# First loads of a convolution/FFN layer on eight cores: a plain first weight tile, 256-token x pieces in turn with weights, and dummy matmuls between

## The chip, the cores and the metric

The kernel runs on all eight cores of one Trainium2 chip. Each core does one layer for one prompt sequence of 2048 tokens and for 16 decode tokens; the cores exchange nothing. The time of a run is that of its slowest core. It is given in microseconds (us). Most executions agree within 0.3%. Some fall into a slow state, in which one die (cores 0 to 3 or 4 to 7) has a lower granted clock. "Granted clock" is the share of TensorE's full clock that the profile shows; "half clock" below is a record of 0.5. Slow runs are left out of every comparison below: medians, ratios and intervals use fast runs alone. PE is TensorE's matmul side in the profile.

## The reference, cut to what matters

The weights are the same for all cores, x is not. The part that matters here is the first feed-forward block, above all its first two products.

```python
D_MODEL, SEQ, D_FF = 1024, 2048, 2816

def swiglu(x, w_gate, w_up, w_down):
    return (jax.nn.silu(x @ w_gate) * (x @ w_up)) @ w_down

def trunk_layer(x, ctx_a, ctx_b, ...):
    x = layer_norm(ALPHA * x + 0.5 * swiglu(x, f1_wg, f1_wu, f1_wd), ...)
    m, new_a, new_b = token_mixers(x, ctx_a, ctx_b, ...)   # needs the carried conv state
    x = layer_norm(ALPHA * x + m, ...)
    x = layer_norm(ALPHA * x + 0.5 * swiglu(x, f2_wg, f2_wu, f2_wd), ...)
    return x, new_a, new_b
```

## The kernel before

All data lie in HBM as f32; matmuls read bf16. In this kernel the loads of x and of the weights that GpSimd issues cast on their way ("casting queue" below). The loads that SyncE issues ("plain queue") land as f32; where bf16 is needed, they land in a stage (a part of the tile `sb_hT` that is not yet in use), and VectorE (DVE) and ScalarE (ACT) cast from there.

The feed-forward block works by weight tile `f` of 128 hidden columns. One tile is 1 MB at the source: 8 KB per partition, the gate half first, then the up half. A tile meets 1024 tokens in two groups of 512; each group is 8 matmuls for the gate and 8 for the up product.

```python
def u_group(idx, b, f, g):                 # [cut to its operations]
    P.op("pe", lambda e: mm(e, 0, bg), reads=[("ring", s, 0)] + xtoks(tok0, n), writes=pst(bg))
    P.op("pe", lambda e: mm(e, 1, bu), reads=[("ring", s, 1)] + xtoks(tok0, n), writes=pst(bu))
    P.op("act", ... Silu ..., writes=[("sg", q)])
    P.op("dve", ... multiply ..., writes=[("hT", f, gi)])
```

Side work (later loads, constants) is woven between the groups by `merge`. It runs a side entry first and then pops as many groups as the gap to the next entry allows:

```python
def merge(items, side):
    credit = 0.0
    for th, gap in side:
        th()
        credit += gap
        while credit >= 1.0 - 1e-9 and items:
            items.pop(0)()
            credit -= 1.0
```

The start of the kernel before, and the load of the carried convolution state (960 KB, plain queue), which waits for a token of tile 1:

```python
first_x(0)              # plain queue: tokens 0..255, 1 MB, cast by DVE and ACT
first_x(1)              # plain queue: tokens 256..511
fetch_wgu(0, 2)         # casting queue: weight tile 0 in two halves
fetch_wgu(1, 2)
fetch_wgu(2)
fetch_xt(0)             # casting queue: tokens 512..1023, 2 MB at the source
fetch_wgu(3)
# [cut] 10 dummy matmuls on zeros, then
u_group(0, 0, 0, (0, 256, 0))
u_group(0, 0, 0, (256, 256, 0))
u_group(1, 0, 1, (0, 512, 0))
u_group(2, 0, 2, (0, 512, 0))
for f in range(3):
    u_group(f, 0, f, (512, 512, 1))
    fetch_wgu(f + NSLOT)
u_group(3, 0, 3, (0, 512, 0))
u_group(3, 0, 3, (512, 512, 1))
# [cut] sample_state(), its first entry:
P.op("sp", lambda e: e.dma_start(out=CA, in_=scat...), reads=[("hT", 1, 1)], writes=["CA"] + ...)
ev = [(0, ss[0]), (1, consts), (18, ss[1]), (22, consts2)] + [(0.5 + 3.0 * i, ... load_wd(0, i)) ...]
merge(up_items(0, 0)[8:], side)
```

## Time and profile before

The first three runs took 1218.16 to 1219.61 us, median 1219.1 us.

| what | value | from |
|---|---|---|
| span of the cores | 1214.0 to 1218.2 us | list of cores |
| PE busy on the slowest core | 98% | page, part 1 |
| start of uninterrupted matmuls, core 1 | 30.2 us | chain of waits |
| real matmul work done by then | 10.4 us | 64 matmuls; 216 ns per 512 columns, 109 per 256 |

The next lines are the chain that ended last on core 1, the slowest, within the first 120 us (start, duration, what). It is read from top to bottom in time.

```profile
4.38 25.60 DMA sb_xT<-xtb
29.98 0.25 issue
30.23 89.87 PE ps L522 x402
```

The 512-token x load, issued at 4.38 us, lands at 29.98 us. From then on PE does not stop. The waits of PE on the same core over the whole run (total us, times, longest) show what else stands in its way; L522 is the matmul of `u_group`, L1115 the dummies, L890 a transpose in the mixer.

```profile
PE ps L522 <- DMA sb_ring<-wgu: 7.5, 2, 7.1
PE ps L522 <- DMA sb_xT<-xtb: 3.2, 1, 3.2
PE ps L1115 <- DVE sb_dgb L1079: 2.4, 1, 2.4
PE ps L890 <- ACT sb_wring L880: 1.1, 1, 1.1
PE ps L522 <- DVE sb_hT L529: 0.5, 1, 0.5
```

All but the last two lie in the first 30 us.

### The profile page before, as it was taken

The page shows a single profiled execution, that of the slowest core. Times are in us where ns is not written, and L with a number is a line of the kernel's source. Part 1 is how long each engine was busy: PE and PEld are TensorE (multiplying, and loading weights), DVE is VectorE, ACT ScalarE, POOL GpSimd, SP SyncE. Part 2 cuts the span into 40 slices and gives each one's busy share as a digit, 9 for nine tenths or more (in the row PEclk, how much of TensorE's full clock was granted, in tenths as well). Part 3 has the DMA queues.
Part 4 walks back from the last instruction along what each step waited for, and adds up shares of the span by engine and source line. Part 5 has one row for each costly group of instructions (what it writes and reads, how often), then busy time and mean ns, then how long its engine had stood idle before and what let it go on. Part 6 is the DMA issues. An engine that isn't in the chain of part 4 may idle for free.

```text
span 1218.2 us, 19722 instructions; the slowest of 8 cores (1214.0 to 1218.2 us)
## 1 busy us (share of the span) xinstructions
PE 1193.5 (98%) x7138; PEld 623.7 (51%) x7138; DVE 539.7 (44%) x885; ACT 238.6 (20%) x420; POOL 198.6 (16%) x310
## 2 busy tenths in 40 slices
PE   5999999999999999999999999999999999999996
PEld 2444444455555556655444444445444466666443
DVE  1123216663433455817864434465736532222365
ACT  1111110121122235411021121235320011211000
POOL 1111112310101013311210100113312110000121
PEclk8999999999999999999999999999999999999999
DMA  9797777766655538994346756438983245443032
GB/s 174 129 190 123 130 152 145 160 145 124 111 107 105 127 69 181 196 218 123 111 112 106 120 98 125 104 84 180 192 199 125 104 102 84 73 70 87 33 106 95
DMA packets 62720, 152.80 MB, mean 125 GB/s; under 512 B 7776, under 2 KB 22304, under 8 KB 62352
## 3 DMA queue, kind: packets, MB, share of 16 engines
q0 software_dynamic: 32944, 79.21, 41.3%
q1 hardware_dynamic: 29680, 72.32, 18.6%
q8 instruction: 59, 0.97, 0.3%
q14 instruction: 37, 0.30, 0.1%
HBM read 202.79 MB, written 28.70 MB: 190 GB/s over the span
## 4 chain that ended last, share of the span: by engine, by line
PE 96%; DMA 2%; DVE 0%; POOL 0%; issue 0%; DVEq 0%; POOLq 0%; ACT 0%; ACTq 0%
PE ps L522 50%; PE ps L586 25%; PE ps L669 12%; PE ps L921 5%; PE ps L773 2%; DMA sb_xT<-xtb 2%; PE ps L411 1%; PE ps L890 1%; PE ps L859 1%; PE ps L592 0%; POOL sb_ring L349 0%; DVEq L165 0%; PE ps L913 0%; POOLq L165 0%; ACT sb_wring L880 0%
## 5 line engine op out<-in xcount | busy, mean ns | idle before, releaser
L522 PE MATMUL ps<-sb_xT,sb_ring 128*128 128x512 bf16 (+3 forms) x3536 | 637.0, 339 | 11.2 <-DMA sb_ring<-wgu 7.5
L522 PEld LDWEIGHTS ps<-sb_xT,sb_ring 128*128 128x128 bf16 x3536 | 344.9, 98 | 284.0 <-issue 22.6
L529 DVE TENSOR_TENSOR sb_hT<-sb_sg,ps 128x512 bf16<-128x512 f32 (+3 forms) x221 | 128.5, 582 | 404.7 <-PE ps L522 394.8
L586 PE MATMUL ps<-sb_RW,sb_hT 128*128 128x512 bf16 x1408 | 306.5, 379 | 0.0
L586 PEld LDWEIGHTS ps<-sb_RW,sb_hT 128*128 128x128 bf16 x1408 | 137.2, 98 | 163.2 <-issue 0.2
L527 ACT ACTIVATE sb_sg<-ps 128x512 f32<-128x512 f32 (+3 forms) x221 | 113.3, 513 | 490.8 <-PE ps L522 440.1
L669 PE MATMUL ps<-sb_xT,sb_wring 128*128 128x512 bf16 (+1 forms) x800 | 149.1, 337 | 0.0
L349 POOL DMA_DIRECT2D sb_ring<-wgu x90 | 49.8, 554 | 480.7 <-PE ps L522 448.9
L669 PEld LDWEIGHTS ps<-sb_xT,sb_wring 128*128 128x128 bf16 x800 | 67.8, 97 | 74.7 <-issue 0.8
L441 POOL TENSOR_SCALAR sb_mv<-sb_mv 128x1 f32<-128x1 f32 (+1 forms) x50 | 44.8, 897 | 350.5 <-DVE sb_mv L439 350.5
L433 DVE SCALAR_TENSOR_TENSOR sb_xr<-sb_xr,ps 128x1024 f32<-128x1024 f32 x47 | 57.3, 1219 | 100.1 <-PE ps L586 87.0
L415 ACT ACTIVATE sb_xT<-ps 128x1024 bf16<-128x1024 bf16 (+1 forms) x34 | 33.1, 980 | 202.7 <-PE ps L411 202.7
L437 DVE BATCH_NORM_STATS2 sb_stt<-sb_xr 128x6 f32<-128x512 f32 (+1 forms) x100 | 64.3, 684 | 5.1
L452 DVE SCALAR_TENSOR_TENSOR sb_xr<-sb_xr,sb_mv,sb_lnb 128x1024 f32<-128x1024 f32 (+1 forms) x33 | 42.4, 1283 | 18.7 <-POOL sb_mv L443 16.3
L449 DVE SCALAR_TENSOR_TENSOR sb_xr<-sb_xr,sb_mv,sb_lnb 128x1024 f32<-128x1024 f32 (+1 forms) x33 | 42.3, 1282 | 1.7
L362 POOL DMA_DIRECT2D sb_wring<-win x40 | 22.0, 551 | 117.4 <-PE ps L669 117.3
L443 POOL TENSOR_TENSOR sb_mv<-sb_mv,sb_neghalf 128x1 f32<-128x1 f32 (+1 forms) x50 | 31.4, 628 | 8.0 <-POOL sb_mv L441 1.4
L686 DVE SCALAR_TENSOR_TENSOR sb_RW<-ps,sb_cst,sb_RW 128x512 f32<-128x512 f32 (+1 forms) x20 | 12.6, 646 | 40.6 <-PE ps L669 40.6
L773 PE MATMUL ps<-sb_RW,sb_dgb 128*32 128x512 bf16 x512 | 30.6, 380 | 0.0
L921 PE MATMUL ps<-sb_wo,sb_RW 128*128 128x512 bf16 x128 | 30.2, 379 | 0.0
L921 PE MATMUL ps<-sb_wo,sb_wring 128*128 128x512 bf16 x128 | 30.2, 379 | 0.0
L897 ACT ACTIVATE sb_wring<-ps,sb_cst 128x128 bf16<-128x128 f32 x64 | 24.1, 458 | 23.9 <-PE ps L890 23.9
(82 smaller groups left out, 457.2 us busy)
## 6 DMA issues: line engine op xcount, KB each, us to landing
sb_ring<-wgu POOLq DMA_DIRECT2D x86, 512.0 KB, 7.0
sb_RW<-wd POOLq DMA_DIRECT2D x33, 512.0 KB, 12.4
sb_wring<-win POOLq DMA_DIRECT2D x40, 256.0 KB, 5.4
sb_RW<-uscr SPq DMA_DIRECT2D x64, 135.0 KB, 6.2
sb_xr<-xp SPq DMA_DIRECT2D x16, 512.0 KB, 8.0
x1s<-sb_xr SPq DMA_DIRECT2D x16, 512.0 KB, 3.5
sb_xr<-x1s SPq DMA_DIRECT2D x16, 512.0 KB, 9.3
x2s<-sb_xr SPq DMA_DIRECT2D x16, 512.0 KB, 8.5
```

The lines of the kernel that those rows point to most:

```text
L349: P.op("pool", lambda e, q=q: e.dma_start(out=ring[:, s, q * m:(q + 1) * m], in_=wgu[w][f][:, q * m:(q + 1) * m], max_dma_last_dim=8192), ...
L433: P.op("dve", lambda e: e.scalar_tensor_tensor(out=xr[:n, s, :], in0=xr[:n, s, :], scalar=in_scale, in1=add, op0=ALU.mult, op1=ALU.add), r ...
L437: P.op("dve", lambda e, h=h: e.bn_stats(out=stt[:n, m, h, :], in_=xr[:n, s, h * 512:(h + 1) * 512]), reads=[("xr", s)], writes=[("stt", m, ...
L441: P.op("pool", lambda e: e.tensor_scalar(out=mv[:n, m, 3:4], in0=mv[:n, m, 1:2], scalar1=eps, scalar2=None, op0=ALU.add), reads=[("mv", m) ...
L452: P.op("dve", lambda e: e.scalar_tensor_tensor(out=xr[:n, s, :], in0=xr[:n, s, :], scalar=mv[:n, m, 2:3], in1=lnb[:n, 1, :], op0=ALU.mult, ...
L522: ins = e.matmul(bank(bk, n), lhsT=ring[:, s, c:c + 128], rhs=xT[:, k, tok0:tok0 + n], start=(k == 0), stop=(k == KC - 1))
L527: P.op("act", lambda e: e.activation(out=sg[:, q, :n], in_=bank(bg, n), func=AF.Silu), reads=pst(bg), writes=[("sg", q)])
L529: P.op("dve", lambda e: e.tensor_tensor(out=hT[:, f, l0:l0 + n], in0=sg[:, q, :n], in1=bank(bu, n), op=ALU.mult), reads=[("sg", q)] + pst( ...
L586: ins = e.matmul(ps[:n, (yb + h) * 512:(yb + h + 1) * 512], lhsT=hT[:, f, l0:l0 + n], rhs=wd[:, f, h * 512:(h + 1) * 512], start=(f == 0), ...
L669: ins = e.matmul(bank(bk, n), lhsT=wring[:, slot, k * 128:(k + 1) * 128], rhs=xT[:, k, tok0:tok0 + n], start=(k == 0), stop=(k == KC - 1))
L773: ins = e.matmul(ps[32 * g_:32 * g_ + 32, bk * 512:(bk + 1) * 512], lhsT=dgb[:, 0, q * 128 + 32 * g_: q * 128 + 32 * g_ + 32], rhs=R2[:, p ...
L921: ins = e.matmul(ps[:n, (4 + h) * 512:(5 + h) * 512], lhsT=lhs(k), rhs=wo[:, k, h * 512:(h + 1) * 512], start=(k == 4), stop=(k == 3))
```

## The change

The intent is to begin real work earlier and to let every landing of 1 MB release more matmuls. The first x piece and the first weight tile come by the plain queue in rows of 8 KB. The other x pieces of the first 1024 tokens are 256 tokens each, in turn with weight tiles. Below, x0 to x3 are these four pieces of x, and w0 to w3 the first four weight tiles. Dummy matmuls (22, then 5 and 5) are to keep the TensorE clock up. Besides, the mixer of block 0 is spaced wider by half a group at three places, and some later loads are shifted.

```diff
-side.append((th, 1.1 if b == 1 and name in ("B6", "B7") else gE if name not in ("B0", "B1") else 0.5 * gE))
+side.append((th, 1.1 if b == 1 and name in ("B6", "B7") else gE if b == 0 or name not in ("B0", "B1") else 0.5 * gE))
 # [cut] the load of the carried state
-reads=[("hT", 1, 1)],
+reads=[("hT", 4, 1)],
 # [cut]
-first_x(0)
-first_x(1)
-fetch_wgu(0, 2)
-fetch_wgu(1, 2)
-fetch_wgu(2)
-fetch_xt(0)
-fetch_wgu(3)
+first()              # plain queue: xta[0], then wgu[0][0]; DVE and ACT cast half of each
+next_x(1)            # casting queue from here on; 256 tokens, 1 MB at the source
+fetch_wgu(1)
+next_x(2)
+fetch_wgu(2)
+next_x(3)
+fetch_wgu(3)
 # [cut]
-10 dummy matmuls
+warm(22)
 u_group(0, 0, 0, (0, 256, 0))
+warm(5)
 u_group(0, 0, 0, (256, 256, 0))
+warm(5)
 u_group(1, 0, 1, (0, 512, 0))
+for f in range(2):
+    u_group(f, 0, f, (512, 256, 1))
 u_group(2, 0, 2, (0, 512, 0))
+u_group(2, 0, 2, (512, 256, 1))
 for f in range(3):
-    u_group(f, 0, f, (512, 512, 1))
+    u_group(f, 0, f, (768, 256, 1))
     fetch_wgu(f + NSLOT)
 # [cut]
-ev = [(0, ss[0]), (1, consts), (18, ss[1]), (22, consts2)] + ...
+ev = [(2, ss[0]), (5, consts), (20, ss[1]), (24, consts2)] + ...
```

## The prediction

> **What bounds the kernel now.** TensorE: the page gives PE 98% busy of 1218.2 us, its chain is 96% PE. Only the start is not PE-bound. The chain of the first 120 us runs from the issue of the 512-token x load (4.38 us; lands at 29.98 us on core 1, 27.6 on cores 0 and 6) straight into uninterrupted matmuls. Before that PE does 64 real matmuls, 10.4 us at full clock (216 ns per 512 columns, 109 per 256). By the waits view of core 1 PE waits 7.1 us (weights), 0.45 (weights), 3.2 (x). The windows view shows the clock at 0.5 from 8.9 to 19.15 and 29.4 to 36.2 us; the matmuls there lost about 3 us each time. So some 23 us of core 1's first 36 us are not work. Core 1 is worst and sets the time (1218.2; the others 1214.0 to 1215.2).
>
> Loads are the limit there: 2 MB of x (plain queue), 3 MB of weights and 2 MB of x (casting queue), counted at the source, at 0.27 to 0.35 MB/us.
>
> **What the change does.**
> 1. First work needs x0 and w0, now both on the plain queue. While both queues run, the packet records show one 8 KB plain packet per 4 KB-source casting packet (27 and 27 in one us). The Trainium skill, "DMA: Bandwidth & Descriptors", section "SWDGE vs HWDGE vs iDMA", says an engine round-robins between the queues; the counts agree. The next x piece's casting packets carry 1 KB of source and take less from the plain queue: w0 should land at 9.5 to 10.5 us (second x piece now: 10.6 to 12.6). Casts: 0.69 us DVE, 1.06 us ACT. First real matmul at about 10.7 us (now 12.1 to 13.9).
> 2. 1 MB pieces in turn: x1 ~13.5, w1 ~16.5, x2 ~21, w2 ~24, x3 ~28, w3 ~31 us. Weights take 3.2 us. An x piece has 1024 packets of 512 B destination: packet times of 300, 154 and 91 ns per queue for 8, 4 and 2 KB of source extrapolate to 60 ns, so 4 us a piece (estimate). Each landing releases more matmuls; the 2 to 3 us wait for the large x load goes.
> 3. 22 dummies, then 5 and 5: the clock rises during the dummies and stays up. The Trainium skill, "TensorE: Matmul & The Clock Gate", Part 1, gives a free-running 3.4 us window; the clock records here step in multiples of 3.41 us. Both half-clock stretches go. Dummies end at 8.7 to 10.4 us and delay nothing.
> 4. Mixer spacing: a 1.1 us wait of PE on ACT at 430 us (all cores) goes.
>
> **Sum.** The first twelve 256-token units end at ~40 us now (core 0; 43.6 core 1); after, ~35 (36.5). Gain 5 to 7 us plus 1.1: about 6 on typical cores, 8 on the slowest.
>
> **Prediction: 1211.5 us, 1207.5 to 1216 in 8 of 10. Faster by over 2%: 0.005; within 2%: 0.985; slower by over 2%: 0.01.**
>
> **Right or wrong shows in:** PE's waits in the first 45 us (none over 2.5 us after the first real matmul, clock never back at 0.5); first real matmul near 10.7; x1 to x3 landing about 7.3 us apart; no ACT wait at 430 us; from 45 to 1200 us only an offset.
>
> **What would make it wrong:** 512 B pieces much slower than 60 ns a packet (at 100 ns x3 lands at 36 us and only the 1.1 us is gained); the casting queue starved until the plain queue ends, so x1 is late; a clock drop in a wait; the slowest core's lag not stemming from its start; later loads (constants, weights f4) pushed into matmuls.

## More of the kernel before

On core 0, the SyncE issues of the first 50 us (start, us, issue):

```profile
1.06 0.86 SPq L1075 DMA_DIRECT2D sb_hT<-xta  x2
1.97 0.43 SPq L1087 DMA_DIRECT2D sb_ident<-ident  x1
37.52 0.69 SPq L1048 DMA_DIRECT2D sb_hT<-scat  x1
```

The program is recorded in order by a helper. `P.op` looks up who wrote each token in `reads`:

```python
def op(self, eng, fn, reads=(), writes=(), dma=None):     # [cut]
    for r in reads:
        w = self.lastw.get(r)
        if w is not None:
            deps[w] = True
```

## The result, and the profile after

The changed kernel took 1216.91 us (median of 4 runs, 1216.82 to 1217.61), the kernel before 1218.63 us in the same rounds. The ratio of fast runs is 0.9986, with a 95% interval of 0.9969 to 1.0003. A ratio is the mean time of one kernel's fast runs over that of the other's of the same rounds, so it is not quite the ratio of the medians quoted. The interval includes 1, so the times alone do not show a gain clear of noise. The gain of 1.7 us by the medians is under a quarter of the 7.6 us that I had predicted, and the time lies outside my range of 1207.5 to 1216.

The slowest core of the profiled run is now core 0. Its chain in the first 120 us (start, duration, what):

```profile
3.23 22.90 DMA sb_xT<-xta
26.14 0.14 issue
26.27 5.32 PE ps L522 x32
```

The chain still goes through an x load: now x2, the piece of tokens 512 to 767. It was issued at 3.23 us and landed at 26.1 us. I had predicted 21. PE's waits on this core over the whole run:

```profile
PE ps L522 <- DVE sb_dummy L339: 4.0, 1, 4.0
PE ps L1125 <- DVE sb_dgb L1088: 2.4, 1, 2.4
PE ps L522 <- DMA sb_xT<-xta: 2.1, 1, 2.1
PE ps L522 <- issue: 0.6, 4, 0.2
PE ps L522 <- DVE sb_hT L529: 0.5, 1, 0.5
PE ps L586 <- issue: 0.5, 3, 0.2
PE ps L890 <- ACT sb_wring L880: 0.3, 1, 0.3
```

The first line is the wait for the first real matmul. The profile names a memset of DVE, but the program makes PE wait for DVE's cast of the first weight tile just before it. The 1.1 us wait of the mixer (L890) is down to 0.3. The matmuls of core 0 in the first 60 us (start, us, operation) show the whole start; L1125 are the dummies.

```profile
2.40 6.90 PE L1125 MATMUL ps<-sb_dgb 128*128 128x512 bf16 x22 [2.40 <-DVE sb_dgb L1088]
13.28 3.56 PE L522 MATMUL ps<-sb_xT,sb_ring 128*128 128x256 bf16 x16 [3.98 <-DVE sb_dummy L339]
16.64 1.28 PE L1125 MATMUL ps<-sb_dgb 128*128 128x512 bf16 x5
17.76 1.91 PE L522 MATMUL ps<-sb_xT,sb_ring 128*128 128x256 bf16 x16
19.72 1.03 PE L1125 MATMUL ps<-sb_dgb 128*128 128x512 bf16 x4
20.58 3.62 PE L522 MATMUL ps<-sb_xT,sb_ring 128*128 128x512 bf16 x16
26.27 34.10 PE L522 MATMUL ps<-sb_xT,sb_ring 128*128 128x256 bf16 x194 [2.07 <-DMA sb_xT<-xta]
```

The first group took 3.56 us in place of 1.91: the clock had fallen after the gap before it (a record of 0.5 from 13.29 to 16.70 us). And here are the SyncE issues of core 0 in the changed kernel:

```profile
1.05 0.40 SPq L1079 DMA_DIRECT2D sb_hT<-xta  x1
1.51 0.42 SPq L1079 DMA_DIRECT2D sb_hT<-wgu  x1
13.45 0.69 SPq L1048 DMA_DIRECT2D sb_hT<-scat  x1
14.19 0.91 SPq L1050 DMA_DIRECT2D sb_CB<-scbt  x1
```

The state load `scat` is issued at 13.45 us and no longer at 37.5. Its gate is `("hT", 4, 1)`. But `merge` pops only one group (tile 4, tokens 0 to 511) ahead of that side entry: the entry before it has a gap of 1.5. When the load is recorded, nobody has written `("hT", 4, 1)`, so it has no such dependency. It goes out as soon as the casts have freed its part of the stage.

### Where the time lies: two numbers per core

I split each core's span at the end of VectorE's multiply for tile 3 on tokens 512 to 1023. At that point both kernels have done the same work. "Start" is the time up to there, "rest" is the span less the start. Start is the median (and maximum) of the eight cores of one profiled run each.

| kernel | start, median (max), us | rest, median, us | span, median, us |
|---|---|---|---|
| before | 47.8 (51.4) | 1166.8 | 1214.5 |
| after | 47.8 (49.7) | 1165.5 | 1213.6 |

The rest is 1.3 us shorter, and on six of the eight cores the figure is 1165.5 or 1165.6. The start, which the change is about, gains nothing at the median.

### The profile page after: what moved, and what is told of

Its sections match the earlier page's. It is cut to its first block, busy times and chain, and to the rows that moved or that the text cites. A ratio compares the mean times of both kernels' runs of the same rounds, so it can differ in the third digit from the quotient of the medians.

```text
span 1215.3 us, 19790 instructions; the slowest of 8 cores (1212.7 to 1215.3 us)
## 1 busy us (share of the span) xinstructions
PE 1190.1 (98%) x7108; PEld 630.5 (52%) x7208; DVE 539.7 (44%) x888; ACT 239.2 (20%) x423; POOL 198.2 (16%) x309
## 3 DMA queue, kind: packets, MB, share of 16 engines
q0 software_dynamic: 34592, 79.21, 42.7%
## 4 chain that ended last, share of the span: by engine, by line
PE 96%; DMA 2%; issue 1%; DVE 0%; POOL 0%; DVEq 0%; POOLq 0%; ACT 0%; ACTq 0%
PE ps L522 50%; PE ps L586 25%; PE ps L669 12%; PE ps L921 5%; PE ps L773 2%; DMA sb_xT<-xta 2%; PE ps L411 1%; PE ps L890 1%; PE ps L859 1%; PE ps L592 0%; DVEq L165 0%; POOL sb_xT L1070 0%; PE ps L913 0%; POOLq L165 0%; ACT sb_wring L880 0%
## 5 line engine op out<-in xcount | busy, mean ns | idle before, releaser
L522 PE MATMUL ps<-sb_xT,sb_ring 128*128 128x352 bf16 (+3 forms) x3544 | 631.4, 336 | 9.1 <-DVE sb_dummy L339 4.0
L522 PEld LDWEIGHTS ps<-sb_xT,sb_ring 128*128 128x128 bf16 x3584 | 349.4, 98 | 272.8 <-issue 13.6
L529 DVE TENSOR_TENSOR sb_hT<-sb_sg,ps 128x352 bf16<-128x352 f32 (+3 forms) x224 | 128.9, 576 | 406.4 <-PE ps L522 396.7
L586 PE MATMUL ps<-sb_RW,sb_hT 128*128 128x512 bf16 x1378 | 302.8, 379 | 1.9 <-issue 0.5
L527 ACT ACTIVATE sb_sg<-ps 128x352 f32<-128x352 f32 (+3 forms) x224 | 113.8, 508 | 485.0 <-PE ps L522 436.7
L669 PE MATMUL ps<-sb_xT,sb_wring 128*128 128x512 bf16 (+1 forms) x780 | 145.2, 336 | 1.2 <-issue 0.2
L349 POOL DMA_DIRECT2D sb_ring<-wgu x87 | 48.1, 553 | 471.5 <-PE ps L522 412.5
L441 POOL TENSOR_SCALAR sb_mv<-sb_mv 128x1 f32<-128x1 f32 (+1 forms) x50 | 44.5, 891 | 350.7 <-DVE sb_mv L439 350.7
L452 DVE SCALAR_TENSOR_TENSOR sb_xr<-sb_xr,sb_mv,sb_lnb 128x1024 f32<-128x1024 f32 (+1 forms) x33 | 42.4, 1284 | 18.5 <-POOL sb_mv L443 16.0
L686 DVE SCALAR_TENSOR_TENSOR sb_RW<-ps,sb_cst,sb_RW 128x512 f32<-128x512 f32 (+1 forms) x20 | 12.6, 646 | 39.9 <-PE ps L669 39.9
## 6 DMA issues: line engine op xcount, KB each, us to landing
sb_RW<-wd POOLq DMA_DIRECT2D x33, 512.0 KB, 13.6
```

Of the source, the lines that this page charges most:

```text
L349: P.op("pool", lambda e, q=q: e.dma_start(out=ring[:, s, q * m:(q + 1) * m], in_=wgu[w][f][:, q * m:(q + 1) * m], max_dma_last_dim=8192), ...
L441: P.op("pool", lambda e: e.tensor_scalar(out=mv[:n, m, 3:4], in0=mv[:n, m, 1:2], scalar1=eps, scalar2=None, op0=ALU.add), reads=[("mv", m) ...
L452: P.op("dve", lambda e: e.scalar_tensor_tensor(out=xr[:n, s, :], in0=xr[:n, s, :], scalar=mv[:n, m, 2:3], in1=lnb[:n, 1, :], op0=ALU.mult, ...
L522: ins = e.matmul(bank(bk, n), lhsT=ring[:, s, c:c + 128], rhs=xT[:, k, tok0:tok0 + n], start=(k == 0), stop=(k == KC - 1))
L527: P.op("act", lambda e: e.activation(out=sg[:, q, :n], in_=bank(bg, n), func=AF.Silu), reads=pst(bg), writes=[("sg", q)])
L529: P.op("dve", lambda e: e.tensor_tensor(out=hT[:, f, l0:l0 + n], in0=sg[:, q, :n], in1=bank(bu, n), op=ALU.mult), reads=[("sg", q)] + pst( ...
```

## The experiments

Theory A: the ungated state load takes turns with the small packets of x2, makes x2 late and eats the gain of the new order. Rival B: x pieces of 512 B packets are slow by themselves. Rival C: the gain is there on typical cores, and a slow core hides it. Further questions were what the dummies, the plain first weight tile, the order and the mixer spacing are worth alone, and why the first weight tile landed late. There were eleven runs, of nine new kernels, one repeat (e10) and the changed kernel once more (e11), all with correct results. Those of one group (e1 to e4, e5 to e8, e9 to e11) ran on one chip and share the runs of the kernel before (medians 1217.73, 1218.53 and 1218.36 us). Every kernel is within 2% of the kernel before; what is compared are differences of a few microseconds.

### e1_gate: the state load gated by a token that exists

```diff
-reads=[("hT", 4, 1)],
+reads=[("hT", 3, 1)],
```

> Only the gate of the sample-state load is changed: it waits for hT of tile 3 (written by then) in place of tile 4 (not yet written in program order, so no wait at all). Theory A (the ungated 0.96 MB load on the plain queue takes turns with the 512 B packets of x2 and makes x2 late): its packets leave the stretch of 17 to 24 us, x2 packets run at 300 or more per us, x2 lands near 20 us in place of 24.4 to 26, PE's wait for it falls from 2 to 4 us to under 0.7, no half-clock stretch near 25 us, the up-stage of the first four weight tiles ends 4 to 6 us earlier (42 to 45.5 us), the time is 1211 to 1212.5. Rival B (x pieces of 512 B packets are slow by themselves): x2 still lands after 23 us, time within 1 us of 1216.9. Rival C (all gains are real but the slowest core hides them): typical cores unchanged at 1213 to 1214.

Measured: 1213.73 us (5 runs), ratio to before 0.9967 (0.9954 to 0.9981). Start 44.8 us (maximum 45.5), rest 1165.5. On core 0 the load is now issued at 45.59 us, x2 lands at 21.9 us in place of 26.1, and PE has no wait for x at all:

```profile
45.59 0.69 SPq L1048 DMA_DIRECT2D sb_hT<-scat  x1
```

```profile
PE ps L522 <- DVE sb_dummy L339: 3.9, 1, 3.9
PE ps L1125 <- DVE sb_dgb L1088: 2.4, 1, 2.4
PE ps L522 <- DVE sb_hT L529: 0.5, 1, 0.5
PE ps L890 <- ACT sb_wring L880: 0.3, 1, 0.3
```

The windows view of core 0 shows the same, first the changed kernel, then this one (stretch, its length, busy us of PE, PEld, DVE, ACT and POOL, granted clock, DMA share, GB/s). PE is idle for most of 23 to 26 us in the first and busy in the second, and the half-clock stretch after 26 us is gone.

```profile
23.00:26.00 3.00, 1.20 (x6) 0.35 (x4) 0.69 (x1) 0.28 (x1) 0.00 (x0) 1.00 1.12 176
26.00:30.00 4.00, 3.73 (x21) 2.81 (x22) 0.42 (x1) 0.38 (x1) 0.00 (x0) 0.62 1.24 173
```

```profile
23.00:26.00 3.00, 3.00 (x26) 2.38 (x25) 1.01 (x2) 0.38 (x1) 0.00 (x0) 1.00 1.25 160
26.00:30.00 4.00, 4.00 (x27) 2.34 (x25) 0.52 (x2) 0.98 (x2) 0.00 (x0) 1.00 0.99 160
```

The packet records of the traces, counted by when they end, show the mechanism. The numbers are packets per us over all 16 engines of core 1.

```
                       512 B (x2, casting queue)   1920 B (state load, plain queue)
after,   17 to 18 us            158 *                        52
after,   18 to 19 us             98                          99
after,   20 to 21 us            110                         116
e1_gate, 17 to 18 us            336                           0
e1_gate, 18 to 19 us            331                           0
         * the state load's packets begin in this microsecond
```

While both queues have work, their packets go one for one (the counts per us do not show the order inside). An x2 packet carries 1 KB of source (512 B of bf16), a state packet 1920 B, so the state load takes nearly two thirds of the source bytes. The gate also holds back the 64 KB load `scbt`, which follows on the same queue; "the state load" below means both. Theory A stands. My size for it was too high: 3.0 us of start at the median, where I expected 4 to 6, and the time is over my 1211 to 1212.5. On the eight cores x2 landed at 20.3 to 22.3 us (24.3 to 26.1 in the changed kernel), where I expected about 20. Rival B falls: in the microseconds in which no other data packets ended, 248 to 348 of the 512 B packets did over the eight cores (in the table, 331 to 336 on core 1). Rival C falls too: the spans of the cores are 1208.3 to 1211.0 us, against 1212.7 to 1215.3.

### e2_before_early: the same fault put into the kernel before

```diff
-reads=[("hT", 1, 1)],
+reads=[],
```

> The kernel before, with the gate of the sample-state load taken out, so that it goes out right after the first casts. Theory A: the same load now takes turns with the packets of the 512-token x load, which lands 2 to 4 us later than 27.6 to 30; the time rises by 2 to 5 us. Rival B: the load does no harm, time unchanged within 1 us.

Measured: 1222.55 us (4 fast runs of 5), ratio 1.0039 (1.0025 to 1.0053), 4.7 us slower by the ratio. Start 52.8 us, which is 5.0 later than before; rest 1166.8, as before. From 21 to 24 us the 1 KB packets of the 512-token x load fell from 144 to 165 per us (means of the three microseconds over the cores, kernel before) to 70 to 81, with 77 to 82 packets of the state load beside them: one for one again. The x load of core 0 took 28.4 us from issue to landing in place of 23.2; over the eight cores it landed 1.7 to 5.2 us later. PE's wait for it on core 0 grew from 2.3 us to this:

```profile
PE ps L522 <- DMA sb_xT<-xtb: 5.5, 1, 5.5
```

In or after that wait the clock fell to 0.5 for 3.4 to 6.8 us on all eight cores; in the kernel before, on four. So the early state load alone costs at least as much in a kernel that has nothing else of the change.

### e3_gate_nodummies: gate mended, no dummies between

```diff
 u_group(0, 0, 0, (0, 256, 0))
-warm(5)
 u_group(0, 0, 0, (256, 256, 0))
-warm(5)
 u_group(1, 0, 1, (0, 512, 0))
```

> The gate mended and both groups of 5 dummy matmuls between the first real groups left out. If these dummies delay real work (two times 1.1 us, on the critical path where the operands have already landed), the start ends up to 2 us earlier than in e1_gate and the time falls by up to 2 us. If they hold the clock up, leaving them out brings a half-clock stretch and costs 1 to 3 us. If PE is waiting for x2 in e1_gate anyway, no change.

Measured: 1211.88 us (1211.78 to 1212.12), ratio 0.9952 (0.9939 to 0.9966). Start 43.3 us, 1.5 under e1_gate. The runs of the two kernels do not overlap (e1_gate: 1212.54 to 1214.16). Core 0 shows why: here are its matmuls in e1_gate, then in this run. In e1_gate each group of dummies stands between the real groups; here the second group starts at 14.24 us and the third at 17.36, both held by loads alone.

```profile
12.97 3.50 PE L522 MATMUL ps<-sb_xT,sb_ring 128*128 128x256 bf16 x16 [3.89 <-DVE sb_dummy L339]
16.30 1.24 PE L1125 MATMUL ps<-sb_dgb 128*128 128x512 bf16 x5
17.38 1.91 PE L522 MATMUL ps<-sb_xT,sb_ring 128*128 128x256 bf16 x16
19.13 1.24 PE L1125 MATMUL ps<-sb_dgb 128*128 128x512 bf16 x5
20.21 30.07 PE L522 MATMUL ps<-sb_xT,sb_ring 128*128 128x512 bf16 x186
```

```profile
11.54 1.91 PE L522 MATMUL ps<-sb_xT,sb_ring 128*128 128x256 bf16 x16 [2.15 <-DVE sb_dummy L339]
14.24 1.91 PE L522 MATMUL ps<-sb_xT,sb_ring 128*128 128x256 bf16 x16 [0.79 <-DMA sb_xT<-xta]
17.36 32.96 PE L522 MATMUL ps<-sb_xT,sb_ring 128*128 128x512 bf16 x199 [1.21 <-DMA sb_ring<-wgu]
```

Part of the difference on this core is that w0 landed 1.4 us earlier in this run; at the median of the cores the first real matmul starts no earlier (12.6 us against 12.4). The dummies between delay real work and do not hold the clock up: without them, four cores show half clock after the 22 dummies. The clock falls earlier than the dummies between, in the gap between the 22 dummies (which end at 9 to 10 us) and the first real matmul: in e1_gate, which has all the dummies, six of eight cores show 3.4 us at 0.5 from 12 to 14 us on. This is the best of the kernels that ran.

### e4_gate_castlate: gate mended, casting queue held until the first weight tile has landed

```diff
 def next_x(j):
     P.op("pool", lambda e: e.dma_start(...),
+         reads=hrow(18) if j == 1 else [],     # written by the load of the first weight tile
          writes=xtoks(256 * j, 256), dma="xta%d" % j)
```

> The gate mended, and the casting queue starts only when the first weight tile has landed. It tells why that tile landed at 11 to 12.3 us where I predicted 9.5 to 10.5. If traffic of the casting queue slows the plain queue, the plain packets keep 0.33 to 0.39 MB/us up to the end, the tile lands at 8 to 9 us and the first real matmul starts at 9 to 10 us; x1 and all later pieces come 0 to 2 us later. If the plain queue slows down by itself from 6 us on (all cores reading at once), the tile still lands after 10.5 us and all later pieces come 3 to 5 us later, the time is 2 to 4 us worse than e1_gate.

Measured: 1218.64 us (3 fast runs of 4), 4.9 us over e1_gate by the medians (5.0 by the ratios), ratio to before 1.0008 (0.9993 to 1.0023). The first real matmul started at 11.2 to 12.4 us (median 11.7) against 11.6 to 13.0 (median 12.4) in e1_gate, so neither of my two branches was right in full. The casting queue cost the first real matmul about 0.7 us at the median. The plain queue has a dip of its own: on cores 1 and 4 it moved 0.25 to 0.33 MB/us from 3 to 6 us, 0.17 to 0.28 from 7 to 9 us and 0.35 to 0.39 from 9 to 10 us, with no casting packet in flight; on cores 0, 2, 5 and 6 it stayed at 0.15 to 0.25 from 7 to 10 us. In e1_gate the dip is the same (0.17 to 0.29 on these cores), and on these two only the last microsecond is slower (0.23 to 0.29 from 9 to 10 us). What makes the dip stays open; the kernel before has it too (0.20 to 0.25 on core 1), where the second plain load is x and not weights. Holding the casting queue back costs more than it frees: the start ends 3.4 us later (48.1).

### e5_longwarm: e3 with 32 dummies at the start

```diff
-warm(22)
+warm(32)
```

> Gate mended, no dummies between, and 32 dummies at the start in place of 22. The clock records of e1_gate show that most cores fall to half clock for one 3.4 us stretch at 12 to 17 us, since the dummies end at 8 to 10 us and the first real matmul starts at 11.6 to 13. If that stretch costs 1.2 to 1.8 us of the slowest core, ten more dummies (2.2 us at full clock) keep the clock up, no core shows 0.5 after it rose, and the time falls by 0.5 to 1.7 us below e3_gate_nodummies (1211.9). If PE waits for the second weight tile at 16 to 17 us anyway, the lost time is hidden and the time does not change.

Measured: 1212.13 us, ratio 0.9951 (0.9938 to 0.9964); e3 had 0.9952 on another chip. No gain; the start of the profiled run, the slowest of the five, ends at 44.5 us at the median. The clock no longer falls before the first real matmul on any core. But PE then stands at the wait for the second weight tile for 1.1 to 2.2 us, and on three cores the clock falls after that wait instead (from 18.4, 18.5 and 20.1 us on). On the five cores where it never falls the start ends at 42.7 to 44.7 us, just the span of e3's eight cores (42.7 to 44.7), four of which had a half-clock stretch. So that stretch seems to have been hidden, for the most part, behind the load.

### e6_before_spacing: the mixer spacing alone, in the kernel before

The edit is the first line of the diff above.

> The kernel before, with the change's mixer spacing alone. The wait of PE on ACT at 430 us falls from 1.1 to 0.3 us as in the changed kernel; the spans fall by 0.8 us on all cores and the time by 0.5 to 1 us. If the spacing does something else to the mixer, other waits appear or the gain is over 1.5 us.

Measured: 1216.35 us (4 fast runs of 5), ratio 0.9982 (0.9968 to 0.9996). Start 47.3, rest 1165.4: the rest is shortened by 1.4 us, just as in the changed kernel. The wait at L890 is no longer in the list of PE's waits on core 6, the slowest:

```profile
PE ps L522 <- DMA sb_ring<-wgu: 7.3, 1, 7.3
PE ps L1115 <- DVE sb_dgb L1079: 2.4, 1, 2.4
PE ps L522 <- DMA sb_xT<-xtb: 2.3, 1, 2.3
PE ps L522 <- DVE sb_hT L529: 0.5, 1, 0.5
```

From matmul start to matmul start the stall was 1.3 us in the kernel before (core 4, at 426 us); the profile's 1.1 counts idle time only. So this one line gives about what the whole change gives (ratio 0.9986).

### e7_oldorder: e3 with the order of before

```diff
 next_x(1)
 fetch_wgu(1)
-next_x(2)
 fetch_wgu(2)
+next_x(2)
 next_x(3)
 fetch_wgu(3)
 # matmuls: tile 2 on tokens 0..511 first, then tiles 0..2 on tokens 512..1023 in groups of 512
```

> As e3_gate_nodummies, but the order of before after the first weights: both weight tiles first, then the x pieces 2 and 3 together, and the matmuls of three weight tiles on the first 512 tokens ahead of the next 512 in one go. If taking x pieces in turn with weights carries the gain, PE waits 2 to 3 us for x3 (landing near 26 us) and may drop to half clock: 1 to 4 us worse than e3_gate_nodummies. If the gain is of the first tile alone, within 0.5 us of e3_gate_nodummies.

Two of four runs were slow; the two fast ones took 1216.60 and 1217.64 us, so there is no interval. The profile of a fast run is clear: start 47.7 us against 43.3 for e3, with a wait for x of 2.2 to 3.9 us on every core; on core 0:

```profile
PE ps L522 <- DMA sb_xT<-xta: 3.5, 1, 3.5
```

The order in turn carries the gain of the start: with the old order it ends where it does in the kernel before, in spite of the plain first weight tile. The order of the loads and that of the matmuls were changed together; which of the two does it was not tested.

### e8_w0cast: e3 with the first weight tile by the casting queue

```diff
-first()              # x0 and the first weight tile plain
-next_x(1)
+first_x(0)           # x0 and x1 plain, as before
+first_x(1)
+fetch_wgu(0, 2)      # first weight tile cast on its way, in two halves
 fetch_wgu(1)
```

> As e3_gate_nodummies, but the first two things on the plain queue are two x pieces, and the first weight tile comes by the casting queue in halves, as in the kernel before; later pieces in turn as in the change. If the plain first weight tile carries a gain, the first real matmul starts at 12 to 15 us in place of 11.5 to 13.5. The second x piece is there at once in exchange, so if the total of loaded bytes up to x2 sets the time, no difference: within 0.7 us of e3_gate_nodummies.

Measured: 1213.44 us (4 fast runs of 5), ratio 0.9956 (0.9942 to 0.9970). Start 44.6 us, 1.3 over e3; the first real matmul at 12.2 to 15.4 us against 11.5 to 13.5. So the plain first weight tile, with x1 on the casting queue in exchange, is worth about 1 us of start in these profiles; the times differ by 0.5 us by the ratios of e8 and e3 (1.0 with e10), inside their intervals, so the size is not shown.

### e9_w0halves, e10_repeat, e11_after: the first tile in two plain loads, with e3 and the changed kernel beside it

```diff
 [in words]
-load of the first weight tile, 8 KB rows
+load of its gate half, 4 KB rows; load of its up half, 4 KB rows
```

> As e3_gate_nodummies, with the first weight tile loaded in two halves on the plain queue, so that its gate half (all that the first eight matmuls read) lands first. If the late first weight tile (first real matmul at 11.5 to 13.5 us) still holds the slowest cores, the first real matmul starts 1 to 2 us earlier and the latest end of the start (44.7 us in e3) falls by 1 us or more, the time by 0.5 to 1.5 us. If the second weight tile at 16 to 17 us is what holds all cores, the time stays within 0.5 us of the repeat beside it.

> e3_gate_nodummies once more, on the same chip and in the same rounds as e9_w0halves and the changed kernel: 1211 to 1212.5 us, 4 to 6 us under the changed kernel.

> The changed kernel as it is, in the same rounds. By theory A its time is 3 to 4 us over e1_gate and 4.5 to 6 us over the repeat, with the 0.96 MB load again between 17 and 24 us and x2 landing after 24 us. If the gain of 1.7 us over the kernel before was all mixer spacing (1.3 us on every core), the median end of the start is again within 0.5 us of that of before, 47.8 us.

Measured: e9 1213.36 us (0.9958; 0.9946 to 0.9970), e10 1212.08 us (5 fast runs of 7; 0.9948; 0.9934 to 0.9961), e11 1217.43 us (4 fast runs of 6; 0.9991; 0.9978 to 1.0005). In e9 the first real matmul starts earlier (median 11.4 us, against 12.4 in e10), but the second half lands later and PE waits for that; the start ends at 44.3 us against 43.4. The rest is longer too (1166.5 us against 1165.6): in the mixer the wait at L890 is 0.7 us on all eight cores, against 0.2 to 0.3 in e10. Why is open. The idea failed. e10 confirms e3. In e11 the start is 48.7 us at the median, a little more than the 0.5 us around 47.8 that I had allowed, and its time is 5.2 us over e10 by the ratios.

### The account

| step | start, median, us | difference |
|---|---|---|
| before (old order, first weight tile cast) | 47.8 | |
| order in turn, 22 dummies, gate mended (e8) | 44.6 | -3.2 |
| + plain first weight tile (e3, e10) | 43.3, 43.4 | -1.3 |
| + dummies between (e1) | 44.8 | +1.5 |
| + gate that waits for nothing (after, e11) | 47.8, 48.7 | +3.0 to +3.9 |

Repeats of one kernel differ by 0.1 to 0.9 us in this figure, so each step is known to about a microsecond at worst. The times support the +1.5 (e1 and e3 do not overlap) and the last step; for the -1.3 they do not decide. The steps are not independent: with the old order the plain first tile gains nothing (e7). The spacing of the mixer gives about 1.3 us outside the start in most kernels that have it (rest 1165.4 to 1165.6 us at the median); in e11 and e9 the rest is 1166.1 and 1166.5.

## Why the prediction was right or wrong

- **The bound: right.** Only the start had time to give.
- **Core 1 "sets the time": wrong as a rule.** In later runs of both kernels the slowest core changes. Its 3.7 us over the median in the one profile before was that run's, and I counted two extra microseconds for it.
- **Step 1, the first weight tile at 9.5 to 10.5 us and the first matmul at 10.7: failed.** The first matmul came at 11.8 to 13.3 us (median 12.7; before 12.1 to 15.3, median 13.6). I took it that smaller packets on the casting queue would leave the plain queue more. But the plain queue's dip from 7 to 9 us does not depend on the other queue (e4_gate_castlate); without any casting packet w0 still landed at 10.2 to 11.4 us. The yardstick was off as well: the prediction has the second plain piece of the kernel before at 10.6 to 12.6 us, the traces have it at 11.6 to 14.5. From there w0 came 1.4 us earlier at the median, as much as forecast. The direction was right; the worth of the step in time is not clear of noise (e8).
- **Step 2, the timetable: right without the state load.** I gave x2 at 21 and x3 at 28 us; e1_gate has 21.9 and 28.3 on core 0. Some of that is luck, since two errors cancelled: w1 landed 0.5 to 1.8 us later than my 16.5, and x2 took 2.9 to 4.2 us after it where I had 4.5. In the changed kernel the step failed, because a load that I had not put into it ran beside it: on core 0 x2 landed at 26.1 and x3 at 32.4 us. The prediction lists later loads (constants, weights) "pushed into matmuls" as a risk. It does not mention the state load, nor ask whether the token of its new gate exists when it is asked for.
- **Step 3, the clock and the dummies: failed in part.** The clock rose during the 22 dummies, but fell again on seven of eight cores, in the gap before the first real matmul or in the wait for x2 (gaps of 2.1 to 4.0 us). "Dummies delay nothing" was wrong for the two groups of 5: they cost 1.5 us of start.
- **Step 4, the mixer: right**, 1.3 us for 1.1, though a wait of 0.3 us is left.
- **The sum: wrong.** The start was to gain 5 to 7 us on typical cores. With the gate mended and without the dummies between it gains 4.4 to 4.5; the dummies take 1.5 of it and the state load 3.0 to 3.9. What was left of the change is the mixer's 1.3 us.

What stays open is why the plain queue dips from 7 to 9 us, and why e9's mixer waits longer.

## What to carry to other kernels

In a stage that waits for loads, count every load that is in flight there, and check when each one really leaves; a gate that names something not yet written is no gate, and nothing complains, since the result is still right. Here two queues shared the engines packet by packet (98 and 99, 110 and 116 per us on core 1), so an unimportant load with large packets took most of the bandwidth from an important one with small packets. Dummy matmuls belong only where PE would stand idle for certain, and a gain in the mean of a change of several parts should be split before it is believed: here one line gave nearly all of it.

## What the Trainium skill lacked or had wrong

- "DMA: Bandwidth & Descriptors", section "Queues, rings and completion order", says that an engine round-robins between queue rows by packet, and that a packet is typically 9 to 17 descriptors. The records agree with taking turns (98 and 99, 110 and 116 per us on core 1): one recorded packet for one in each us; the order inside was not looked at. The page does not say what follows for the bytes: beside 1920 B packets, a stream of 512 B packets (1 KB at the source) falls from 331 to 336 per us to about 100 (core 1).
- The same page, in "Specifications", gives a first-byte latency of about 1 us for loads from GpSimd. The traces show more, counted from the start of the issuing instruction (the page does not say from where it counts): the first casting packet started 4.3 to 6.2 us after its issue in the kernel before, with the plain queue busy, and 1.8 to 3.3 us after it in e4_gate_castlate, with nothing else in flight. It gives about 0.6 us for SyncE; the first load of the kernel before took 1.0 to 1.2 us, the state load of the changed kernel 4.3 to 4.8.
- "TensorE: Matmul & The Clock Gate", Part 1, was borne out in the window's length: every half-clock stretch that the records of the starts show is 3.41 us or a multiple (6.83, 10.24). What decides whether a gap brings one is not read off its length here: one of 2.0 us was enough (core 6 of the kernel before), one of 3.1 us was not (core 7 of the changed kernel). That such a stretch can be hidden behind a load (e5_longwarm: none before the first real matmul, no gain) no page says.
- No page says what makes a plain load of 8 KB rows dip from 0.25 to 0.33 MB/us (3 to 6 us) to 0.17 to 0.28 (7 to 9 us), with all eight cores loading and no casting packet in flight (e4_gate_castlate, cores 1 and 4).
